# Gated columns' loads and first products half a column sooner, and the last tile's parts reordered at the entry of the up projection

## Chip, core and metric

The kernel runs on one core of a Trainium2 chip. The metric is device time in microseconds (us) of one execution; lower is better. The kernel before takes 1490.2 us, the median of three runs (1489.46 to 1492.07).

## What is computed

One encoder layer over 1024 tokens (two sequences of 512) of width 1024, in fp32. A projection of the normalised input gives attention heads, a state-space branch and two gates; the two branches are merged through the gates and projected, and a squared-ReLU MLP follows:

```python
y_att = windowed_attention(q, k, v, sink, bias, band_mask(seq_len))
y = jax.nn.gelu(lax.map(one_seq, u))                  # state-space branch
y_ssm = y * jax.nn.sigmoid(y @ w_glu + b_glu)
mixed = jax.nn.sigmoid(g_att) * y_att + jax.nn.sigmoid(g_ssm) * y_ssm
x = x + mixed @ w_out
h2 = rms_norm(x, ln2)
return x + jnp.square(jax.nn.relu(h2 @ w_up)) @ w_down
```

The change lies in two places: where `mixed` is made, and at the seam between `mixed @ w_out` with its norm and `h2 @ w_up`.

## The kernel before, in words

Every fp32 matmul is made of three: each operand is split into a high part (a cast to the matmul's format, on ScalarE, ACT) and a low part (what the cast left, a subtraction on VectorE, DVE). `mm3` (L113 to L117) multiplies high by high, high by low and low by high. A part is thus always a pair: an ACT cast, then a DVE subtraction that waits for it. TensorE is PE; its weight loads are PEld.

**The order.** From L1200 to L1714 the order of PE, ACT, DVE and GpSimd (POOL) is the order in which the program calls them (`written`). Each engine works its own queue in that order, and an instruction that waits holds back all behind it on its engine. The DMA issues of SyncE (SP) in this stretch are put in order by a scheduler, which issues a load when the tile that it writes comes free.

**The gated columns** (L1395 to L1461). The merge goes over eight columns m of 128 features, each in two halves s of 512 tokens. Column 0 is done ahead of the loop. For m = 1 to 7:

- `col.multiply` is 24 PE matmuls of y with column m of w_glu for half s (L758). At s = 0 of columns 2 to 6, `column_parts(m + 1)` splits the next column's weights, in two pieces: cast c_hi (L741) and subtraction c_lo (L742). Their raw pieces come by DMA (L740) into two buffers.
- `bank_out(m, s)` is ACT's sigmoid of the product (L1415).
- `late()` is the `mix` of the half before: DVE makes z (L1421, a product with the gate's tile gs, and L1422, the sum with at), ACT casts it into mixT (L1424), DVE subtracts (L1425). mixT is the moving side of the w_out projection that follows.
- `gate_in(m)` at s = 0: ACT's sigmoid of gs (L1409), DVE's product of gs with y (L1410, tile yr) and of at with ga (L1411), each over both halves.
- `loads(m + 1)` at s = 1 fetches the four tiles gs, yr, ga and at of the next column, 512 KB each (L1398, L1400, L1402, L1404). gs and yr have two buffers each, ga and at share four. So a tile of column m + 1 lands in the buffer of column m - 1: gs when L1421 of mix(m - 1, 1) is done, at when L1422 is, yr and ga when L1410 and L1411 of gate_in(m - 1) are.
- From m = 5 on, pieces of w_out are loaded (L1383) and split (cast L1391, subtraction L1392).

The last mix but one, mix(7, 0), makes the last eighth of what block 0 of the w_out projection reads (`Rows.block`, L1492, matmuls of 256 columns at L115 to L117).

**The entry of the up projection** (L1678 to L1718). The MLP's up projection is a product of 2 x 2 blocks in seven multiplications (Strassen's scheme in Winograd's form): B11, B21, B22 and T1 to T4 are blocks, or sums of blocks, of the normalised rows, and sums of blocks of w_up are their partners. Rows come in tiles of 128; the last of them (`last`) is normalised and transposed (`norm`, `turn`) while PE works on two products of r = 0 and two of r = 1 that need only B11 and B21, each 12 matmuls of 512 columns. Then PE multiplies, for r = 0, in this order: T2 with made[2], T3 with made[3], T1 with made[1], B22 with made[4], T4 with the raw block (L1795 to L1815). `put` writes a tile's part of one of the blocks (cast L1479, subtraction L1480), `parts` makes a pair of weight parts (u_hi, L1671; u_lo, L1672). Before the change, `last.old_rows()` (two sums, L1549), `first_sum` (copy L1657, sum L1659, relu, square) and the two sums of weights (L1696, L1697) come first; then `sums_a` casts B22, T1 and T2 and subtracts their low parts in this order, `between` makes made[2] and begins made[3], and T3, T4, made[1] and made[4] follow.

Of the kernel before, what the change touches and what calls it, by code (L numbers as in the profile page):

```python
# [23 lines left out]
KT = D // P  # L24
# [39 lines left out]
def hybrid_layer(ctx, tc, x, xT, rel, onehot, early, w_qkv, w_ug, q_gain, k_gain, sink,  # L64
# [1330 lines left out]
    with tc.tile_pool(name="glu", bufs=2, reuse_waits="tile") as gpool:  # L1395
# [11 lines left out]
        def gate_in(m):  # L1407
            gs_, yr, ga, at = gated[m]
            S.activation(gs_, gs_, AF.Sigmoid)  # L1409
            V.tensor_mul(gs_, gs_, yr)  # L1410
            V.tensor_mul(at, at, ga)  # L1411
# [25 lines left out]
        for m in range(1, KT):  # L1437
            col = ahead if m == 1 else Column(m)
            for s in range(NSEQ):
                col.multiply(max((s + 1) * 3 * KT - col.i, 0))  # L1440
                if s == 0 and 1 < m < KT - 1:
                    w_g[m + 1], subs = column_parts(m + 1)
                    for sub in subs:
                        sub()
                ending = m == KT - 1 and s
                if ending:
                    late()
                gl = bank_out(m, col.ps[s])
                if not ending:
                    late()  # L1450
                if s == 0:
                    gate_in(m)
                elif m < KT - 1:
                    gated[m + 1] = loads(m + 1)
                late = lambda m=m, s=s, gl=gl: mix(m, s, gl)
                if m >= 5:
                    n = (m - 5) * 2 + s
                    load_piece(n)
                    if 1 <= n < 5:
                        split_piece()  # L1460
# [17 lines left out]
    def put(dst, src, cs, at_once=True):  # L1478
        S.copy(dst[0][:, :, cs], src)  # L1479
        sub = lambda: V.tensor_sub(dst[1][:, :, cs], src, dst[0][:, :, cs].bitcast(F32))  # L1480
        return sub() if at_once else sub

    class Rows:
# [59 lines left out]
        def temp(self, name):  # L1543
            return rn2.tile([P, 4, P], F32, tag=name, name=name)

        def old_rows(self):
            self.s11, self.s21 = self.temp("s11"), self.temp("s21")
            for dst, (hi, lo) in ((self.s11, B11), (self.s21, B21)):
                V.tensor_add(dst, hi[:, :, self.cs].bitcast(F32), lo[:, :, self.cs].bitcast(F32))  # L1549

        def sums_a(self, between=None):
            cs, (x12, x22) = self.cs, self.xb
            b22 = put(B22, x22, cs, False)
            self.x22 = self.temp("x22")
            S.copy(self.x22, x22)
            self.t1, self.t2 = self.temp("tt0"), self.temp("tt1")
            V.tensor_sub(self.t1, x12, self.s11)
            t1 = put(T1, self.t1, cs, False)
            V.tensor_sub(self.t2, x22, self.t1)
            t2 = put(T2, self.t2, cs, False)  # L1560
            b22()
            t1()
            t2()
            if between:
                between()
            V.tensor_sub(self.t1, self.x22, x12)
            self.t3 = put(T3, self.t1, cs, False)

        def sums_b(self):
            self.t3()  # L1570

        def sums_c(self):
            V.tensor_sub(self.t2, self.t2, self.s21)
            put(T4, self.t2, self.cs)

    x1_all = slot_b.tile([P, NT // 2, D], F32, tag="act0", name="x1_all")
    with tc.tile_pool(name="wout", bufs=1, reuse_waits="tile") as wb:
# [30 lines left out]
        for t in range(1, 4):  # L1608
# [4 lines left out]
            if t > 1:  # L1613
                rows1[t - 2].sums_b()
                rows1[t - 2].sums_c()
            old.old_rows()
            old.norm()
            old.turn()
            add = rows1[t].half(1)
# [26 lines left out]
    def product(ps, w, b):  # L1646
        for k in range(4):
            mm3(ps, [q[:, k, :] for q in w], [q[:, k, :] for q in b], k == 0, k == 3)
        return ps

    def put_a(n, r, src):

        S.dma_start(a_scr[n - 1, :, r, :], src)

    def first_sum(r, p1, p2):
        u1 = up1.tile([P, HALF], F32, tag="u1", name="u1")
        S.copy(u1, p1)  # L1657
        a11 = up1.tile([P, HALF], F32, tag="a11", name="a11")
        V.tensor_add(a11, p2, u1)  # L1659
        S.activation(a11, a11, AF.Relu)  # L1660
        S.activation(a11, a11, AF.Square)
        put_a(1, r, a11)
        return u1, a11

    def sum_tile(i):
        return up1.tile([P, 4, P], F32, tag=f"s{i}", name=f"s{i}", bufs=1)
# [10 lines left out]

    begun, made = {}, {}  # L1678
    last = rows1[3]
    p1 = product(acc(), first[0][0], B11)  # L1680
    add()
    rows1[2].sums_b()
    rows1[2].sums_c()
    p2 = product(acc(), first[0][1], B21)
    last.norm()
    subs = [first_parts(up_raws[1][:, i], first[1][i]) for i in range(2)]
    for sub in subs:
        sub()
    last.old_rows()
    last.turn()  # L1690
    begun[0] = first_sum(0, p1, p2)
    p1 = product(acc(), first[1][0], B11)
    p2 = product(acc(), first[1][1], B21)
    a11_, a12_, a21_, a22_ = [up_raws[0][:, i] for i in range(4)]
    sm = [sum_tile(i) for i in range(4)]
    V.tensor_add(sm[0], a21_, a22_)  # L1696
    V.tensor_sub(sm[1], sm[0], a11_)  # L1697

    def between():
        made[2], sub = parts(sm[1], False)  # L1700
        sub()
        V.tensor_sub(sm[2], a11_, a21_)
        made[3], sub = parts(sm[2], False)
        last.sub3 = sub

    last.sums_a(between)
    last.sums_b()
    last.sub3()
    last.sums_c()
    made[1] = parts(sm[0])  # L1710
    V.tensor_sub(sm[3], a12_, sm[1])
    made[4] = parts(sm[3])
    begun[1] = first_sum(1, p1, p2)
    written.__exit__(None, None, None)  # L1714
    rn2_cm.__exit__(None, None, None)
    wb0_cm.__exit__(None, None, None)
# [265 lines left out]
```

## Time and profile before

| | |
|---|---|
| median of three runs | 1490.2 us (1489.46 to 1492.07) |
| the profiled execution | 1493.12 us, of which span 1491.3 us |
| PE busy | 1458.9 us, 98% of the span, 8070 matmuls |
| DVE busy | 1096.3 us, 74% |
| ACT busy | 764.2 us, 51% |
| gated columns' matmuls (L758), m = 1 to 7 | to 767.1 us |
| w_out projection and norm | 767.1 to about 884 us |
| up projection | from about 884 us |

Times in the trace count from the span's start. A row of the timeline has start, duration, engine, line, operation, the tile written and the tiles read (out<-in), the shapes, and in brackets the engine's idle time before it with what ended it. A wait row has total, number and longest. A row of the windows has the stretch, its length, each engine's busy time, the granted TensorE clock (1.00 is full speed), the DMA engines' mean busy share and the GB/s moved. Matmuls overlap in their rows: what counts is the distance from one start to the next.

### The profile page before, as it was taken

The page shows a single profiled execution, that of the slowest core. Times are in us where ns is not written, and L with a number is a line of the kernel's source. Part 1 is how long each engine was busy: PE and PEld are TensorE (multiplying, and loading weights), DVE is VectorE, ACT ScalarE, POOL GpSimd, SP SyncE. Part 2 cuts the span into 40 slices and gives each one's busy share as a digit, 9 for nine tenths or more (in the row PEclk, how much of TensorE's full clock was granted, in tenths as well). Part 3 has the DMA queues.
Part 4 walks back from the last instruction along what each step waited for, and adds up shares of the span by engine and source line. Part 5 has one row for each costly group of instructions (what it writes and reads, how often), then busy time and mean ns, then how long its engine had stood idle before and what let it go on. Part 6 is the DMA issues. An engine that isn't in the chain of part 4 may idle for free.

```text
span 1491.3 us, 22155 instructions
## 1 busy us (share of the span) xinstructions
PE 1458.9 (98%) x8070; PEld 1251.9 (84%) x8070; DVE 1096.3 (74%) x1835; ACT 764.2 (51%) x1366; POOL 168.4 (11%) x270
## 2 busy tenths in 40 slices
PE   6999999999999999999999999999999999999998
PEld 5888888888998888987879978888888888888787
DVE  7799979964637888888873689777777588575553
ACT  5589852224427777786433345555545543433332
POOL 4111120000322333333000100000000000000000
PEclk9999999999999999999999999999999999999999
DMA  8355566358841313236854125544443794454441
GB/s 297 109 177 172 173 214 234 133 180 282 269 119 56 100 58 93 74 127 232 274 199 144 71 96 181 161 151 153 155 155 127 269 350 161 148 181 154 127 126 59
DMA packets 129241, 243.91 MB, mean 164 GB/s; under 512 B 16059, under 2 KB 59323, under 8 KB 129132
## 3 DMA queue, kind: packets, MB, share of 16 engines
q1 hardware_dynamic: 104684, 186.87, 39.7%
q10 hardware_dynamic: 21888, 46.15, 8.2%
q0 software_dynamic: 2560, 9.48, 1.9%
q8 instruction: 64, 1.05, 0.3%
q14 instruction: 45, 0.37, 0.1%
HBM read 173.20 MB, written 81.82 MB: 171 GB/s over the span
## 4 chain that ended last, share of the span: by engine, by line
PE 81%; DVE 8%; issue 4%; ACT 3%; DMA 2%; POOL 1%; SPq 0%; DVEq 0%; ACTq 0%; POOLq 0%
PE bank L117 13%; PE bank L116 13%; PE bank L115 13%; PE acc L146 11%; PE acc L729 7%; PE acc L115 3%; PE acc L117 3%; PE acc L116 3%; PE sps L609 2%; PE sps L865 2%; PE sps L1053 2%; PE po L1085 2%; PE tps L1069 1%; DVE p L1057 1%; PE lag L624 1%
## 5 line engine op out<-in xcount | busy, mean ns | idle before, releaser
L116 PE MATMUL bank<-b_lo,a_hi 128*128 128x512 f32 x440 | 171.6, 390 | 1.9 <-DVE b_lo L1858 1.9
L117 PE MATMUL bank<-b_hi,a_lo 128*128 128x512 f32 x440 | 171.3, 389 | 0.0
L115 PE MATMUL bank<-b_hi,a_hi 128*128 128x512 f32 x440 | 170.7, 389 | 0.0
L729 PE MATMUL acc<-w_hi,hT 128*128 128x256 f32 x768 | 165.0, 292 | 0.0
L146 PE MATMUL acc<-hT,c_hi 128*128 128x512 f32 x512 | 161.2, 395 | 0.0
L1857 ACT CAST a_hi<-d_a 128x1024 fp32r<-128x1024 f32 x55 | 57.9, 1053 | 180.9 <-PE bank L116 177.7
L1858 DVE TENSOR_TENSOR a_lo<-d_a,a_hi 128x1024 fp32r<-128x1024 f32 x55 | 67.3, 1224 | 101.9 <-ACT a_hi L1857 99.9
L729 PEld LDWEIGHTS acc<-w_hi,hT 128*128 128x128 f32 x768 | 126.8, 190 | 1.7
L146 PEld LDWEIGHTS acc<-hT,c_hi 128*128 128x128 f32 x512 | 94.6, 188 | 21.1 <-issue 2.5
L729 PE MATMUL acc<-w_lo,hT 128*128 128x256 f32 x384 | 108.3, 282 | 0.0
L115 PE MATMUL bank<-act,u_hi 128*128 128x512 f32 x256 | 99.8, 390 | 1.1 <-ACT u_hi L1671 1.1
L146 PE MATMUL acc<-hT,c_lo 128*128 128x512 f32 x256 | 100.3, 392 | 0.0
L117 PE MATMUL bank<-act,u_lo 128*128 128x512 f32 x256 | 99.9, 390 | 0.2
L116 PE MATMUL bank<-act,u_hi 128*128 128x512 f32 x256 | 99.9, 390 | 0.1
L116 PEld LDWEIGHTS bank<-b_lo,a_hi 128*128 128x128 f32 x440 | 82.6, 188 | 19.8 <-DVE b_lo L1858 2.7
L117 PEld LDWEIGHTS bank<-b_hi,a_lo 128*128 128x128 f32 x440 | 82.6, 188 | 17.1
L115 PEld LDWEIGHTS bank<-b_hi,a_hi 128*128 128x128 f32 x440 | 82.6, 188 | 17.1
L1063 ACT ACTIVATE p<-p,nmx 128x257 f32<-128x257 f32 (+1 forms) x128 | 72.3, 565 | 35.9 <-DVE nmx L1057 35.4
L729 PEld LDWEIGHTS acc<-w_lo,hT 128*128 128x128 f32 x384 | 73.1, 190 | 2.4
L1057 DVE CUSTOM_DVE_ANT_0 p<-sps,bias,nsink 128x256 f32<-128x256 f32 (+1 forms) x128 | 69.2, 541 | 3.9 <-DMA bias<-line_scr 1.3
L115 PE MATMUL acc<-w,act 128*128 128x256 f32 (+1 forms) x224 | 68.8, 307 | 1.9 <-ACT act L1424 1.9
L1671 ACT CAST u_hi<-s 128x512 fp32r<-128x512 f32 x64 | 39.4, 622 | 60.6 <-PE bank L116 44.0
(369 smaller groups left out, 3737.5 us busy)
## 6 DMA issues: line engine op xcount, KB each, us to landing
d_a<-a_scr SPq DMA_DIRECT2D x55, 512.0 KB, 3.6
u_raw<-in_w_up_dram SPq DMA_DIRECT2D x32, 512.0 KB, 5.8
a_scr<-t ACTq DMA_DIRECT2D x64, 256.0 KB, 2.1
k<-in_w_down_dram SPq DMA_DIRECT2D x32, 512.0 KB, 5.6
a_scr<-a ACTq DMA_DIRECT2D x48, 256.0 KB, 3.3
c_raw<-in_w_ug_dram SPq DMA_DIRECT2D x44, 256.0 KB, 3.4
ct_scr<-ctab SPq DMA_DIRECT2D x16, 576.0 KB, 3.3
ctab_in<-ct_scr SPq DMA_DIRECT2D x32, 288.0 KB, 4.7
```

Source lines behind the costliest of these rows:

```text
L115: PE.matmul(ps, a[0], b[0], start=first, stop=False)
L116: PE.matmul(ps, a[0], b[1], start=False, stop=False)
L117: PE.matmul(ps, a[1], b[0], start=False, stop=last)
L146: PE.matmul(self.ps[s], self.w[p == 2][:, k, :], hT[s][p == 1][:, k, :], start=i % (3 * KT) == 0, stop=i % (3 * KT) == 3 * KT - 1)
L609: PE.matmul(ps[:, i * P:(i + 1) * P], bm[:, ri, g, :], u_sb[:, g, :], start=True, stop=True)
L729: PE.matmul(ps, act[p == 2][:, k, col:col + P], self.w[k // 4][p == 1][:, k % 4, :], start=i == 0, stop=i == 3 * KT - 1)
L865: PE.matmul(o, ctab[:, ri, gi, 0:T * CH], st[:, ri, g].rearrange("p s k -> p (s k)"), start=False, stop=ri == 1)
L1057: V.tensor_tensor_reduce(self.p[:, h, 1:1 + self.nk], self.s[h][:, 0:self.nk], biases[self.j][h][:, b0:b0 + self.nk], -1.0, nsink[:, hh:hh ...
L1063: S.activation(p, p, AF.Exp, bias=self.nmx[:, h:h + 1], scale=-1.0, accum_out=self.sums[:, h, self.qb:self.qb + 1])
L1671: S.copy(hi, src)
L1857: S.copy(hi, src)
L1858: V.tensor_sub(lo, src, hi.bitcast(F32))
```

## The change

In the gated columns, `gate_in(m + 1)` moves to s = 1 of column m (column 1 keeps its place, and column 2's follows half a column later), and `loads(m + 1)` to s = 0. At the entry of the up projection, the last tile's sums and parts are written out by hand in the order in which PE reads them: T2 and made[2] first, then T3 and made[3], T1 and made[1], B22, then T4 and made[4]. The sum sm[0] goes ahead of the low part of T4 of the tile before, ReLU and square of r = 0 and the copy of r = 1's first product go behind B22's cast, and the two sums of `old_rows` are apart, s11 for T2 early and s21 for T4 late. x22 is copied out of PSUM after T2's cast, and B22's part is made from the copy.

```diff
@@ -1449,9 +1449,12 @@
                 if not ending:
                     late()
                 if s == 0:
-                    gate_in(m)
+                    if m == 1:
+                        gate_in(1)
+                    if m < KT - 1:
+                        gated[m + 1] = loads(m + 1)
                 elif m < KT - 1:
-                    gated[m + 1] = loads(m + 1)
+                    gate_in(m + 1)
                 late = lambda m=m, s=s, gl=gl: mix(m, s, gl)
                 if m >= 5:
                     n = (m - 5) * 2 + s
@@ -1543,12 +1546,14 @@
         def temp(self, name):
             return rn2.tile([P, 4, P], F32, tag=name, name=name)
 
-        def old_rows(self):
-            self.s11, self.s21 = self.temp("s11"), self.temp("s21")
-            for dst, (hi, lo) in ((self.s11, B11), (self.s21, B21)):
+        def old_rows(self, *which):
+            for i in which:
+                name, (hi, lo) = (("s11", B11), ("s21", B21))[i]
+                dst = self.temp(name)
+                setattr(self, name, dst)
                 V.tensor_add(dst, hi[:, :, self.cs].bitcast(F32), lo[:, :, self.cs].bitcast(F32))
 
-        def sums_a(self, between=None):
+        def sums_a(self):
             cs, (x12, x22) = self.cs, self.xb
             b22 = put(B22, x22, cs, False)
             self.x22 = self.temp("x22")
@@ -1561,17 +1566,15 @@
             b22()
             t1()
             t2()
-            if between:
-                between()
             V.tensor_sub(self.t1, self.x22, x12)
             self.t3 = put(T3, self.t1, cs, False)
 
         def sums_b(self):
             self.t3()
 
-        def sums_c(self):
+        def sums_c(self, at_once=True):
             V.tensor_sub(self.t2, self.t2, self.s21)
-            put(T4, self.t2, self.cs)
+            return put(T4, self.t2, self.cs, at_once)
 
     x1_all = slot_b.tile([P, NT // 2, D], F32, tag="act0", name="x1_all")
     with tc.tile_pool(name="wout", bufs=1, reuse_waits="tile") as wb:
@@ -1613,7 +1616,7 @@
             if t > 1:
                 rows1[t - 2].sums_b()
                 rows1[t - 2].sums_c()
-            old.old_rows()
+            old.old_rows(0, 1)
             old.norm()
             old.turn()
             add = rows1[t].half(1)
@@ -1652,15 +1655,25 @@
 
         S.dma_start(a_scr[n - 1, :, r, :], src)
 
-    def first_sum(r, p1, p2):
+    def first_copy(p1):
         u1 = up1.tile([P, HALF], F32, tag="u1", name="u1")
         S.copy(u1, p1)
+        return u1
+
+    def first_sum(r, p1, p2):
+        return first_rest(r, first_copy(p1), p2)()
+
+    def first_rest(r, u1, p2):
         a11 = up1.tile([P, HALF], F32, tag="a11", name="a11")
         V.tensor_add(a11, p2, u1)
-        S.activation(a11, a11, AF.Relu)
-        S.activation(a11, a11, AF.Square)
-        put_a(1, r, a11)
-        return u1, a11
+
+        def rest():
+            S.activation(a11, a11, AF.Relu)
+            S.activation(a11, a11, AF.Square)
+            put_a(1, r, a11)
+            return u1, a11
+
+        return rest
 
     def sum_tile(i):
         return up1.tile([P, 4, P], F32, tag=f"s{i}", name=f"s{i}", bufs=1)
@@ -1677,40 +1690,59 @@
 
     begun, made = {}, {}
     last = rows1[3]
+    a11_, a12_, a21_, a22_ = [up_raws[0][:, i] for i in range(4)]
+    sm = [sum_tile(i) for i in range(4)]
     p1 = product(acc(), first[0][0], B11)
     add()
     rows1[2].sums_b()
-    rows1[2].sums_c()
+    t4_put = rows1[2].sums_c(False)
+    V.tensor_add(sm[0], a21_, a22_)
+    t4_put()
     p2 = product(acc(), first[0][1], B21)
     last.norm()
     subs = [first_parts(up_raws[1][:, i], first[1][i]) for i in range(2)]
     for sub in subs:
         sub()
-    last.old_rows()
+    V.tensor_sub(sm[1], sm[0], a11_)
+    u1 = first_copy(p1)
     last.turn()
-    begun[0] = first_sum(0, p1, p2)
+    made[2], made2 = parts(sm[1], False)
+    last.old_rows(0)
+    x12, x22 = last.xb
+    cs = last.cs
+    tt0, tt1 = last.temp("tt0"), last.temp("tt1")
+    V.tensor_sub(tt0, x12, last.s11)
+    V.tensor_sub(tt1, x22, tt0)
+    t2 = put(T2, tt1, cs, False)
+    rest0 = first_rest(0, u1, p2)
+    made2()
+    t2()
     p1 = product(acc(), first[1][0], B11)
     p2 = product(acc(), first[1][1], B21)
-    a11_, a12_, a21_, a22_ = [up_raws[0][:, i] for i in range(4)]
-    sm = [sum_tile(i) for i in range(4)]
-    V.tensor_add(sm[0], a21_, a22_)
-    V.tensor_sub(sm[1], sm[0], a11_)
-
-    def between():
-        made[2], sub = parts(sm[1], False)
-        sub()
-        V.tensor_sub(sm[2], a11_, a21_)
-        made[3], sub = parts(sm[2], False)
-        last.sub3 = sub
-
-    last.sums_a(between)
-    last.sums_b()
-    last.sub3()
-    last.sums_c()
-    made[1] = parts(sm[0])
+    x22c = last.temp("x22")
+    S.copy(x22c, x22)
+    V.tensor_sub(sm[2], a11_, a21_)
+    V.tensor_sub(last.s11, x22c, x12)
+    made[3], made3 = parts(sm[2], False)
+    t3 = put(T3, last.s11, cs, False)
+    made3()
+    t3()
+    t1 = put(T1, tt0, cs, False)
+    made[1], made1 = parts(sm[0], False)
+    t1()
+    made1()
+    b22 = put(B22, x22c, cs, False)
+    begun[0] = rest0()
+    u1 = first_copy(p1)
+    last.old_rows(1)
+    b22()
+    V.tensor_sub(tt1, tt1, last.s21)
+    t4_put = put(T4, tt1, cs, False)
     V.tensor_sub(sm[3], a12_, sm[1])
-    made[4] = parts(sm[3])
-    begun[1] = first_sum(1, p1, p2)
+    made[4], made4 = parts(sm[3], False)
+    t4_put()
+    made4()
+    begun[1] = first_rest(1, u1, p2)()
     written.__exit__(None, None, None)
     rn2_cm.__exit__(None, None, None)
     wb0_cm.__exit__(None, None, None)
```

The subtraction order of the other tiles is as it was; `old_rows(0, 1)` there makes both sums.

## The prediction

> **What bounds the kernel now.** I read the page first, then the waits of PE, then windows and the timeline at the two places where PE waits inside the changed code, and last the DMA issues there. The page gives the span; the profiled execution took 1493.12 us, 1.8 us more than its span and 2.9 us more than the median 1490.2 of the three timed runs. I take the gains and losses in microseconds from this execution and apply them to the median.
>
> ```profile
> span 1491.3 us, 22155 instructions
> ```
>
> PE is the bound almost everywhere. Asked for PE's waits between 690 and 800 us, and between 865 and 925 us, the trace names three, and these are all the changed code can win back:
>
> ```profile
> PE acc L115 <- ACT act L1424: 1.9, 1, 1.9
> PE acc L116 <- DVE w L1392: 1.7, 1, 1.7
> ```
> ```profile
> PE bank L115 <- ACT u_hi L1671: 1.1, 1, 1.1
> ```
>
> The first two lie at one place, the entry of the w_out projection. The windows there (span, PE busy, granted clock, DMA share, GB/s) and PE's timeline show that the place costs more than the waits:
>
> ```profile
> 769.40:773.60 4.20, 0.64 (x4) 0.93 0.20 44
> 773.60:779.80 6.20, 6.15 (x27) 0.50 0.97 364
> ```
> ```profile
> 767.11 0.28 PE L115 MATMUL acc<-w,act 128*128 128x256 f32 x1
> 767.22 0.28 PE L116 MATMUL acc<-w,act 128*128 128x256 f32 x1
> ...
> 779.85 0.28 PE L115 MATMUL acc<-w,act 128*128 128x256 f32 x1
> ```
>
> The projection starts at 767.11, and its 49th matmul at 779.85. The trace has 0.12 us from one such matmul to the next at full clock, so 48 of them are 5.76 us and the 49th was due at 772.87: 6.98 us are lost. 3.6 us are the two waits. After them 27 matmuls run from 773.65 to 779.85 at a clock of 0.50: 6.20 us where 27 x 0.12 = 3.24 would do, 2.96 us more. The remaining 0.4 us is the restart around each wait. So the lost clock is nearly half of the loss, and it follows a stretch of 4.2 us in which PE worked 0.64 us.
>
> What ends last there is the chain of DVE and ACT through the gated columns. This is half a round of it, for m = 5 (the row with x2 is two instructions):
>
> ```profile
> 742.61 1.29 DVE L742 TENSOR_TENSOR c_lo<-c_raw,c_hi 128x512 fp32r<-128x512 f32 x2
> 743.81 1.14 DVE L1421 TENSOR_TENSOR z<-gl,gs 128x512 f32<-128x512 f32 x1
> 744.98 0.69 DVE L1422 TENSOR_TENSOR z<-z,at 128x512 f32<-128x512 f32 x1
> 746.36 0.69 DVE L1425 TENSOR_TENSOR act<-z,act 128x512 fp32r<-128x512 f32 x1 [0.69 <-ACT act L1424]
> 747.32 1.23 DVE L1410 TENSOR_TENSOR gs<-gs,yr 128x1024 f32<-128x1024 f32 x1 [0.27 <-ACT gs L1409]
> 748.47 1.22 DVE L1411 TENSOR_TENSOR at<-at,ga 128x1024 f32<-128x1024 f32 x1
> 749.60 1.14 DVE L1421 TENSOR_TENSOR z<-gl,gs 128x512 f32<-128x512 f32 x1
> ```
> ```profile
> 772.98 0.62 ACT L1424 CAST act<-z 128x512 fp32r<-128x512 f32 x1 [4.25 <-DVE z L1422]
> ```
>
> DVE's idle in it is the 0.69 us of each mix and 0.27 us before L1410, both inside fixed sequences; it never waits for PE. DVE runs late on its own work, and PE gets the last hi part at 773.60.
>
> **Part 1, the gated columns.** Nothing is added or removed; gate_in(m + 1) (one ACT sigmoid, L1410, L1411) moves from behind mix(m, 1) to behind mix(m, 0), and the four loads from (m, 1) to (m, 0). All seven gate_in still stand ahead of mix(7, 0) on DVE, each behind an L1425 as now, with the same 0.27 us of waiting for the sigmoid. So the length of DVE's chain up to L1424 at 772.98 is the same sum in another order: worth 0.0 us by itself. The earlier product buys nothing, because DVE has no hole that it could fill.
>
> What the move does change is what stands behind gate_in. From L1425 at 746.36 to L1421 at 749.60 are 3.24 us; L742's two halves start 0.60 apart, and L1425 has their shape, so gate_in takes 3.24 - 0.60 = 2.64 us. The weight parts c_lo of the next column now stand behind it and come 2.64 us later. Column 4 has the least room:
>
> ```profile
> 722.31 1.28 DVE L742 TENSOR_TENSOR c_lo<-c_raw,c_hi 128x512 fp32r<-128x512 f32 x2
> ```
> ```profile
> 724.04 0.39 PE L758 MATMUL acc<-act,c_lo 128*128 128x512 f32 x1
> ```
>
> Its first half is done at 722.31 + 0.69 = 723.00 and is read at 724.04: 1.04 us of room, so PE waits 2.64 - 1.04 = 1.6 us there, a wait that is not in the trace of before. It costs nothing in the end: PE arrives at 767.11 + 1.6 and stands so much less at the entry, since the chain's end is fixed. Bounds: 0 to 1.6 us, taken as 0 net.
>
> The loads have a price. gs(m + 1) can be fetched only when L1421 of mix(m - 1, 1) has freed its buffer; call that L1421's start t. Now L1409 of gate_in(m + 1) wants it after mix(m - 1, 1) and mix(m, 0): the next L1421 at t + 3.15 (746.36 + 0.60 - 743.81), L1422 1.17 later, L1424 0.73 after that, L1409 0.52 behind it: t + 5.57. SP's queue of before, near the same rows:
>
> ```profile
> 743.32 0.94 SPq L740 DMA_DIRECT2D c_raw<-in_w_glu_dram  x2
> 744.98 0.33 SPq L1398 DMA_DIRECT2D gs<-gs_scr  x1
> 745.70 0.33 SPq L1404 DMA_DIRECT2D at<-mix_scr  x1
> 748.58 0.32 SPq L1400 DMA_DIRECT2D yr<-y_scr  x1
> 749.71 0.32 SPq L1402 DMA_DIRECT2D ga<-ga_scr  x1
> ```
> ```profile
> DMA to landing us min/median/max: 3.4/4.3/4.7
> ```
>
> The second fence is L1398's landing. The SP issues stand in the order in which DVE frees the buffers: yr and ga behind L1410 and L1411, c_raw behind L742, gs and at behind L1421 and L1422. With gate_in moved, L1410 ends at t - 1.20 - 1.13 - 1.15 + 1.23 = t - 2.25, so yr and ga of the column after go out just ahead of c_raw and gs instead of 4 us behind them, on the same queue: 0.524 x 4 = 2.10 MB up to the end of gs. The rates of full stretches:
>
> ```profile
> 704.00:712.00 8.00, 8.00 (x37) 6.63 (x36) 7.13 (x9) 2.25 (x4) 1.22 (x2) 1.00 0.96 297
> 712.00:716.00 4.00, 4.00 (x19) 3.31 (x18) 3.28 (x3) 0.76 (x2) 3.16 (x2) 1.00 0.92 352
> ```
>
> Their last two columns are DMA share and GB/s. The fastest landing, 3.4, less 0.524 MB at 352 GB/s (1.5 us) leaves 1.9 us fixed. So gs lands at t - 2.2 + 1.9 + 6.0 = t + 5.7 at 352 GB/s, or t + 6.8 at 297: 0.1 to 1.2 us after L1409 wants it. Behind L1409 wait L741, the next sigmoid and L1424 on ACT, L1410, c_lo and the mix on DVE, and PE for c_lo. This meets gate_in(3) to gate_in(6); gate_in(2) has its gs from 704, and for gate_in(7) a split piece gives 0.6 us and no c_raw is left. Four times 0.1 to 1.2 is 0.4 to 4.8 us; below nothing it cannot be, as a load cannot speed up DVE. I take 0.3 each, nearer to the row of 352 since the other shares the engines with a POOL load: **+1.2 us**.
>
> [...]
>
> **Part 2, the up half's entry.** PE should go on from 883.42 at 0.23 us a matmul:
>
> ```profile
> 883.42 0.39 PE L117 MATMUL acc<-act,f 128*128 128x512 f32 x1
> 884.94 0.49 PE L115 MATMUL bank<-act,u_hi 128*128 128x512 f32 x1 [1.13 <-ACT u_hi L1671]
> ...
> 889.69 0.39 PE L115 MATMUL bank<-act,u_hi 128*128 128x512 f32 x1
> ```
> ```profile
> 883.02 0.69 DVE L1559 TENSOR_TENSOR tt<-sps,tt 128x512 f32<-128x512 f32 x1 [0.91 <-ACT x L1555]
> 883.63 0.68 DVE L1480 TENSOR_TENSOR act<-sps,act 128x512 fp32r<-128x512 f32 x1
> 884.23 1.28 DVE L1480 TENSOR_TENSOR act<-tt,act 128x512 fp32r<-128x512 f32 x2
> 885.43 0.68 DVE L1672 TENSOR_TENSOR u_lo<-s,u_hi 128x512 fp32r<-128x512 f32 x1
> ```
>
> Sixteen steps from 883.42 to 889.69 take 6.27 us instead of 3.63 (0.227 each, the pace of the rows around): 2.64 us lost, in the first product's T2 and u parts and in the second's u_lo. B22 and T1, which are used third and fourth, stand ahead of T2 on DVE. Now they go behind. The new order counted from here:
>
> ```profile
> 875.89 1.28 DVE L1528 SCALAR_TENSOR_TENSOR rn_xn<-x,rs,ln_bc 128x1024 f32<-128x1024 f32 x1
> 877.09 1.29 DVE L1476 TENSOR_TENSOR f<-u_raw,f 128x512 fp32r<-128x512 f32 x2
> 878.29 1.29 DVE L1549 TENSOR_TENSOR s<-act,act 128x512 f32<-128x512 f32 x2
> ```
>
> The norm stays at 875.89, as sm[0] fills the wait for T4's cast ahead of it. From 878.29 at 0.60 each: sm[1], s11, tt0, tt1 (880.1), a11, u_lo (881.3), T2's lower part at 881.9, done at 882.6. ACT's casts, 0.62 each, follow sm[1] at 879.0 and tt1 at 880.8, in time for both. PE wants them at 883.65: 1.0 us of cover. The second product needs T3 and its u_lo at 886.4; sm[2], the T3 sum, u_lo and T3's lower part with one cast between end at about 885.2. So the whole loss goes: **-2.6 us** (bounds 0 and -2.6). relu and square of a11 and the copy of p1 go behind on ACT; their readers come after the first products. What is late next is made[4] for the fourth product, done near 890.2 and wanted at 891.8.
>
> **Sum.** -2.6 + 0.0 + 1.2 = -1.4 us: 1491.7 by the profiled execution, 1488.8 by the median. About 0.2%, 3.0 us, is what a measurement of this kernel can tell from no change, so this is no change.
>
> **The rivals.** *The clock stays whole (faster).* If gs lands in time, PE's 1.6 us at column 4 shrink the standing at the entry from two waits to one of about 2 us: L116's split, ready at 771.2, is met at 767.11 + 1.6 + 19 x 0.12 = 771.0. For it speaks that the stop of 1.5 us at 883.42 left the pace at 0.23; against it that less than 1 us of lateness closes it again, since lateness pushes the chain's end and PE alike. Then the 2.96 us of half clock go: -2.6 - 3.0 = -5.6, **1484.6**. Chance 0.36.
>
> [...]
>
> *The loads come late (slower).* At 297 GB/s gs is 1.2 us late four times, and mix_scr's store of 0.5 MB falls among the loads of gate_in(3), 1.8 us more: +6.6 - 2.6 = +4.0, **1494.2**. It decides from 5.6 us of lateness in all. For it speaks the median landing of 4.3 with only c_raw ahead; against it the row of 352. Chance 0.18.
>
> *The entry does not clear.* Were ACT late with T2 by over 1 us, PE's wait stays: -1.4 + 2.6 = +1.2, **1491.4**. The cover of 1.0 us speaks against it. Chance 0.04. My forecast has 0.42.
>
> **The numbers.** Faster by over 0.2% (below 1487.2) is the first rival and a little of the forecast where the loads come near the lower bound: 0.37. Within: the rest of the forecast and the third rival: 0.45. Slower: 0.18. The forecast's own range is 1487.2 to 1491.2 (lateness 0 to 3.6 us). Both signs hold much of the chance, so the range takes in the first rival to 0.8 us below and most of the second: 1483.8 to 1493.8.
>
> **What would show it.** Right: no wait for u_hi L1671 near 884 and the second product at 0.23 us a matmul; idle of DVE before L1410 grown from 0.27 to about 0.6; PE waits for c_lo L742 at the columns' starts; the clock at 0.50 again behind the entry. The first rival: a clock of 1.00 there. The second: idle before L1410 over 1.5. The prediction is wrong if DVE's chain from L1410 of m = 1 to the last L1424 gets shorter than now without a change of the clock.

## The result and the profile after

The changed kernel takes 1496.52 us, the median of five runs (1495.46 to 1498.10); the kernel before, run beside it, 1490.87 (1489.46 to 1495.11). The ratio is 1.0035, with a 95% interval of 1.0023 to 1.0048: slower, by 0.0035 x 1490.87 = 5.2 us. The profiled execution took 1498.1 us, and its span is 5.0 us longer than that of before:

```profile
span 1496.3 us, 22154 instructions
```

Both traces hold the same 8070 matmuls in the same order, so the start of each can be taken from its start in the other. The changed kernel is 1.3 us ahead when the gated columns begin, 4.6 behind once column 3 runs, 4.3 behind after the entry of w_out, 1.6 behind after the up half's entry, 4.0 behind at the end of the up projection, and 5.0 behind at the end. (The last 1.0 us arises in the down projection, at one wait that moved from kernel to kernel below by 0.8 us the one way to 1.3 the other, with the same code there; I do not put it down to the change.) So the gated columns lost 5.6 us, the up half's entry won 2.7, and r = 1 gave 2.4 of it back.

PE's waits of the changed kernel, asked for 690 to 800 us (the four longest) and for 800 to 940 us:

```profile
PE acc L758 <- DVE c_lo L742: 3.9, 1, 3.9
PE acc L115 <- ACT act L1424: 1.9, 1, 1.9
PE acc L115 <- ACT w L1391: 0.6, 1, 0.6
PE acc L116 <- DVE w L1392: 0.4, 1, 0.4
```
```profile
PE bank L115 <- ACT u_hi L1684: 1.2, 1, 1.2
PE bank L117 <- DVE u_lo L1685: 0.7, 1, 0.7
```

The entry of w_out still has its wait for L1424. New is a stop of 3.9 us in the columns, for c_lo. The waits near 884 us are gone; the two in the second fence stand at 902, in r = 1.

**The gated columns.** DVE's timeline where the stop arises (start, duration; the bracket is the idle time ahead):

```profile
703.42 1.22 DVE L1410 TENSOR_TENSOR gs<-gs,yr 128x1024 f32<-128x1024 f32 x1
...
711.17 1.22 DVE L1410 TENSOR_TENSOR gs<-gs,yr 128x1024 f32<-128x1024 f32 x1 [2.25 <-DMA yr<-y_scr]
712.31 3.36 DVE L1411 TENSOR_TENSOR at<-at,ga 128x1024 f32<-128x1024 f32 x1
715.60 1.28 DVE L742 TENSOR_TENSOR c_lo<-c_raw,c_hi 128x512 fp32r<-128x512 f32 x2
```

This is gate_in(2). c_lo of column 3, which in the kernel before ran ahead of all this, starts at 715.60. What gate_in(2) waits for is in the rows of ACT, SP and POOL:

```profile
710.08 1.06 ACT L1409 ACTIVATE gs<-gs 128x1024 f32<-128x1024 f32 x1 [1.89 <-DMA gs<-gs_scr]
```
```profile
703.53 0.33 SPq L1398 DMA_DIRECT2D gs<-gs_scr  x1
```
```profile
703.27 1.22 POOL L1119 DMA_DIRECT2D fac<-rs_scr  x2 [5.55 <-DMA rs_scr<-row]
711.28 3.31 POOL L1124 TENSOR_TENSOR ya<-ya,fac 128x1024 f32<-128x1024 f32 x1 [6.80 <-DMA fac<-rs_scr]
```

gs(2) is issued at 703.53 and lets the sigmoid start at 710.08, 6.5 us later, beside POOL's loads of fac. Then L1411 runs into POOL's product at 711.28 and takes 3.36 us instead of 1.22. This meeting is not new: in the kernel before POOL's product met L1422, which took 2.65 us instead of 0.69:

```profile
712.56 2.65 DVE L1422 TENSOR_TENSOR z<-z,at 128x512 f32<-128x512 f32 x1
```

So it costs the chain 2.1 us instead of 2.0. What is new is that c_lo of column 3 stands behind it, and behind the late gs.

The columns behind it wait too; here is gate_in(5):

```profile
744.98 1.06 ACT L1409 ACTIVATE gs<-gs 128x1024 f32<-128x1024 f32 x1 [0.87 <-DMA gs<-gs_scr]
```
```profile
738.29 1.13 DVE L1421 TENSOR_TENSOR z<-gl,gs 128x512 f32<-128x512 f32 x1
...
746.08 1.22 DVE L1410 TENSOR_TENSOR gs<-gs,yr 128x1024 f32<-128x1024 f32 x1 [1.24 <-ACT gs L1409]
```

Its gs was issued at 739.45, which is 36.0 us behind the first L1410. In the kernel before the same load went out 30.1 us behind it (734.83 against 704.76), with 11.4 us to go until its sigmoid; now there are 5.5:

```profile
739.45 0.32 SPq L1398 DMA_DIRECT2D gs<-gs_scr  x1
```
```profile
734.83 0.33 SPq L1398 DMA_DIRECT2D gs<-gs_scr  x1
```

So the change made this load later, not sooner: its buffer comes free behind L1421 of mix(3, 1), and gate_in(4) now stands ahead of that.

Over all columns, the idle time of DVE ahead of L1410, after and then before:

```profile
  ACT gs L1409: 4.3, 5
  DMA yr<-y_scr: 2.3, 1
```
```profile
  ACT gs L1409: 1.6, 6
```

That is 6.6 us against 1.6. (The trace puts the 2.25 us of column 2 down to yr, but yr(2) was issued at 694.46, and the sigmoid of gs ended at 711.14, just ahead of L1410 at 711.17; in kernel 1 below the same wait is named gs, with 2.61.) The chain ends here, in ACT's row of mix(7, 0):

```profile
777.22 0.62 ACT L1424 CAST act<-z 128x512 fp32r<-128x512 f32 x1 [2.57 <-DVE z L1422]
```

From the first L1410 to this row are 777.22 - 703.42 = 73.80 us. In the kernel before the first L1410 is

```profile
704.76 1.22 DVE L1410 TENSOR_TENSOR gs<-gs,yr 128x1024 f32<-128x1024 f32 x1
```

and the row of the prediction ends the chain at 772.98: 68.22 us. The chain is 5.6 us longer, 5.0 of it idle time ahead of L1410. The windows of the changed kernel (span, busy time and count of PE, PEld, DVE, ACT, POOL, then granted clock, DMA share, GB/s) show the two stops and the clock behind each:

```profile
711.60:716.30 4.70, 0.74 (x2) 0.30 (x2) 4.70 (x4) 1.15 (x3) 3.77 (x2) 0.95 0.46 177
716.30:719.40 3.10, 3.07 (x8) 2.45 (x9) 2.38 (x4) 0.76 (x2) 0.00 (x0) 0.52 1.01 309
...
772.90:777.90 5.00, 2.10 (x15) 1.49 (x13) 3.60 (x6) 1.82 (x4) 0.00 (x0) 0.94 0.32 86
777.90:784.10 6.20, 6.20 (x27) 5.98 (x28) 4.69 (x7) 2.19 (x4) 0.00 (x0) 0.50 0.94 365
```

**The up half's entry.** PE's rows:

```profile
887.66 0.39 PE L117 MATMUL acc<-act,f 128*128 128x512 f32 x1
887.89 0.39 PE L115 MATMUL bank<-act,u_hi 128*128 128x512 f32 x1
...
892.65 0.39 PE L115 MATMUL bank<-act,u_hi 128*128 128x512 f32 x1
```
```profile
901.26 0.39 PE L117 MATMUL bank<-t,f_lo 128*128 128x512 f32 x1
902.81 0.50 PE L115 MATMUL bank<-act,u_hi 128*128 128x512 f32 x1 [1.16 <-ACT u_hi L1684]
903.15 0.39 PE L116 MATMUL bank<-act,u_hi 128*128 128x512 f32 x1
904.21 0.50 PE L117 MATMUL bank<-act,u_lo 128*128 128x512 f32 x1 [0.67 <-DVE u_lo L1685]
```

The first products run on at 0.23 us a matmul. Five products later PE stops for r = 1's u_hi. On ACT this cast stands behind f_hi, the first part of r = 2, which waits for its load:

```profile
901.62 0.62 ACT L1478 CAST f_hi<-u_raw 128x512 fp32r<-128x512 f32 x1 [4.46 <-DMA u_raw<-in_w_up_dram]
902.14 1.65 ACT L1684 CAST u_hi<-s 128x512 fp32r<-128x512 f32 x3
```

In the kernel before the two stood in the same order, but the wait was short:

```profile
896.95 0.62 ACT L1475 CAST f_hi<-u_raw 128x512 fp32r<-128x512 f32 x1 [0.73 <-DMA u_raw<-in_w_up_dram]
```

The load waits for its buffer, until f_lo of r = 0 has read it: f_lo ran at 892.40 before and at 895.74 after, and the load went out at 893.11 and at 896.46. PE is 1.6 us behind there, so against PE part 2 itself sent this load 1.75 us later.

### The profile page after: what moved, and what is told of

The parts are those of the page before. It is cut to its first block, busy times and chain, and to the rows that moved or that the text cites. A ratio compares the mean times of both kernels' runs of the same rounds, so it can differ in the third digit from the quotient of the medians.

```text
span 1496.3 us, 22154 instructions
## 1 busy us (share of the span) xinstructions
PE 1462.2 (98%) x8070; PEld 1253.6 (84%) x8070; DVE 1096.5 (73%) x1835; ACT 764.7 (51%) x1366; POOL 169.2 (11%) x270
## 4 chain that ended last, share of the span: by engine, by line
PE 81%; DVE 8%; DMA 4%; issue 3%; ACT 2%; POOL 1%; SPq 0%; DVEq 0%; ACTq 0%; POOLq 0%
PE bank L117 13%; PE bank L116 13%; PE bank L115 13%; PE acc L146 11%; PE acc L729 7%; PE acc L115 3%; PE acc L117 3%; PE acc L116 3%; PE sps L609 2%; PE po L1085 2%; PE sps L1053 2%; PE sps L865 2%; PE tps L1069 2%; PE lag L624 1%; DMA gs<-gs_scr 1%
```

## The experiments

Each kernel ran in five rounds against the kernel before on the same chip; the medians of before are 1491.6, 1491.7 and 1491.7 us in the three groups. Intervals are 95%.

**Theory and rivals.** Theory A: part 1 loses because gs lands late, most of all for column 2, and DVE's chain grows by the waits; part 2 wins at its place and gives the gain back in r = 1. Rival B: the sooner order or the sooner loads cost by themselves. (In the expectations of kernels 1 to 3 the letter B stands for other rivals, which are told there.) Later came theory C against D, on why part 2 gives its gain back, and E and G, on the entry of w_out.

**1. Part 1 alone** (the first hunk of the change).

> Gated columns moved, entry of the up projection as before. Theory A (gs lands after its sigmoid wants it, first at gate_in(2), then at gate_in(4) to gate_in(6); the weight parts of column 3 stand behind that): all of the changed kernel's loss is here, 1490.9 + 5.5 = about 1496.4, PE's wait for c_lo at column 3 near 4 us, and L1424's last hi part about 5.5 us later than in the kernel before. Theory B (the loss comes from the new order at the up projection's entry and after it): 1490.9 to 1491.5, and the chain's end where it was.

Measured: 1498.49 us, ratio 1.0039 (1.0025 to 1.0053). The stop at column 3 is 3.9 us again, and L1409's waits for its load in this kernel are

```profile
  DMA gs<-gs_scr: 4.4, 4
```

Part 1 makes the whole loss, 5.8 us.

**2. Part 2 alone** (all other hunks).

> Gated columns as before, entry of the up projection in the new order. Theory A (the 2.6 us won at the entry are given back at r = 1, where the casts u_hi stand on ACT behind a cast that waits for the load of r = 2): -2.6 + 2.1 = -0.5, about 1490.4, with one PE wait of about 1.2 for u_hi some 15 us behind the entry. Theory B (that wait comes from the gated columns' lateness and not from the new order): -2.6, about 1488.3, without that wait.

Measured: 1492.31 us, ratio 1.0000 (0.9991 to 1.0009): nothing, though the up half's entry wins 2.7 us in the trace. PE's waits between 860 and 940 us and ACT's rows there:

```profile
PE bank L115 <- ACT u_hi L1681: 2.0, 1, 2.0
PE bank L117 <- DVE u_lo L1682: 0.7, 1, 0.7
```
```profile
895.47 0.62 ACT L1475 CAST f_hi<-u_raw 128x512 fp32r<-128x512 f32 x1 [5.36 <-DMA u_raw<-in_w_up_dram]
895.99 1.66 ACT L1681 CAST u_hi<-s 128x512 fp32r<-128x512 f32 x3
```

r = 2's f_hi waits 5.36 us ahead of r = 1's casts. Behind the 2.0 and 0.7 us the matmuls go at 0.43 us from 898.06 to 901.05, at a mean granted clock of 0.73 over 896 to 901, so r = 1 gives back 4.9 us in this one execution, more than the two waits and more than the 2.7 won; over all executions part 2 comes out even.

**3. Part 1 with column 2 at its old place.**

```diff
                 if s == 0:
-                    gate_in(m)
-                elif m < KT - 1:
-                    gated[m + 1] = loads(m + 1)
+                    if m <= 2:
+                        gate_in(m)
+                    if m < KT - 1:
+                        gated[m + 1] = loads(m + 1)
+                elif 1 < m < KT - 1:
+                    gate_in(m + 1)
```

> Gated columns moved but for column 2, whose gate_in stays at its old place; entry of the up projection as before. Theory A: the 2.0 us of DVE at gate_in(2) and PE's stop of 4 us at column 3 with the halved clock are gone, and 0.9 us each at gate_in(4) to gate_in(6) stay, with 0.1 us more between mixes: chain +3.4, about 1494.2. Theory B (gate_in(2) with its stop is the whole loss, the later loads are hidden): about 1490.9.

Measured: 1495.27 us, ratio 1.0022 (1.0013 to 1.0032). The stop at column 3 is gone; two columns still wait, 2.4 us for gs in all. Column 2 carries somewhat under half of the loss.

**4. The calls of the loads half a column sooner, every gate_in at its old place.**

```diff
                 if s == 0:
                     gate_in(m)
-                elif m < KT - 1:
-                    gated[m + 1] = loads(m + 1)
+                    if m < KT - 1:
+                        gated[m + 1] = loads(m + 1)
```

> Only the loads are called half a column sooner; gate_in and the entry as before. Theory A (loads cost only where the products wait for them): the chain's end where it was, 1490.9 within 0.5. Theory B (the bunched loads themselves take bandwidth or SP's queue from c_raw and w_raw): at least 1 us slower, 1492 or more, with ACT waiting for DMA at L741 or L1391.

Measured: 1491.68 us, ratio 1.0005 (0.9996 to 1.0014). L1409 never waits for its load. But the loads themselves do not go out sooner, because each still waits for its buffer. This is gs(6), 40.13 us behind the first L1410 (703.88); in the kernel before it stands 40.22 behind it:

```profile
744.01 0.33 SPq L1398 DMA_DIRECT2D gs<-gs_scr  x1
```

Of the loads of the four tiles behind the first L1410 only at(3) moves by more than 0.2 us, by 2.0. So this kernel shows that moving the calls alone moves next to nothing. What sooner loads cost it does not show; that half of rival B is met by kernel 7.

**5. Part 2 alone, with r = 2's first part held behind r = 1's casts.** One ACT copy of four columns ties f_hi of r = 2 to the third of the parts that r = 1 makes; the real cast overwrites it.

```diff
-        def raw_parts(src):
+        def raw_parts(src, after=None):
...
+            if after is not None:
+                S.copy(hi[:, 0, 0:4], after[:, 0, 0:4])
...
-                u1, a11 = first_sum(r, product(bank(), raw_parts(raw[:, 0]), B11), product(bank(), raw_parts(raw[:, 1]), B21))
+                u1, a11 = first_sum(r, product(bank(), raw_parts(raw[:, 0], mark if r == 2 else None), B11), product(bank(), raw_parts(raw[:, 1]), B21))
...
-            p5 = product(bank(), w1(), T1)
+            w1p = w1()
+            mark = w1p[0]
+            p5 = product(bank(), w1p, T1)
```

> Kernel: the one before with part 2 alone (as in the run of part 2 alone), and the first parts of r = 2 held behind r = 1's own casts by one added ACT copy of 4 columns, so that the load of u_raw(2) no longer stands in ACT's and DVE's queues ahead of u_hi and u_lo of r = 1. Theory C (part 2 gains its 2.5 us at the entry and gives it back only because f_hi of r = 2 waits 5.36 us for its load ahead of the three u_hi casts): the ACT wait for u_raw ahead of u_hi is gone, the PE waits at r = 1's p6 (2.0 and 0.7 us, and the halved clock behind them) go, and the gain stays: 1488 to 1489.5, ratio 0.9975 to 0.9990, faster. Rival D (r = 1's parts are late for their own reasons, DVE and ACT being full behind the entry): PE waits of 1 to 3 us at the same place and 1491 to 1492.5, ratio 0.9995 to 1.001.

Measured: 1488.73 us, ratio 0.9982 (0.9973 to 0.9991). ACT's rows have changed places:

```profile
892.60 1.66 ACT L1681 CAST u_hi<-s 128x512 fp32r<-128x512 f32 x3 [0.45 <-ACT a L1669]
...
897.10 0.62 ACT L1475 CAST f_hi<-u_raw 128x512 fp32r<-128x512 f32 x1 [2.60 <-DMA u_raw<-in_w_up_dram]
```

The load is still waited for, but by nobody whom PE needs, and PE has no wait between 860 and 940 us. Theory C holds.

**6. Part 1 with a third buffer for gs.** ga and at share three buffers instead of four to make room.

```diff
-            gs_ = evp.tile([P, T, NSEQ, NCHUNK], F32, tag="ev", name="gs")
+            gs_ = (gpool if m % 3 == 2 else evp).tile([P, T, NSEQ, NCHUNK], F32, tag="g3" if m % 3 == 2 else "ev",
+                                                      name="gs", bufs=1 if m % 3 == 2 else 2)
...
-            ga = gpool.tile([P, NTOK], F32, tag="ga", name="ga", bufs=4)
+            ga = gpool.tile([P, NTOK], F32, tag="ga", name="ga", bufs=3)
...
-            at = gpool.tile([P, NTOK], F32, tag="ga", name="at", bufs=4)
+            at = gpool.tile([P, NTOK], F32, tag="ga", name="at", bufs=3)
```

> Kernel: the one before with part 1 alone, and a third buffer for gs (the ga and at loads share three buffers instead of four to make room), so that no gs load has to wait for the last reader of gs two columns back. Theory A (part 1 loses because gs lands late, most of all for column 2): the sigmoid L1409 waits for no DMA (under 0.3 us in each column, instead of 2.25, 1.12, 0.56 and 0.50), the PE stop of 3.9 us ahead of column 3 is at most 1 us, and the time is back at that of the kernel before or a little under it: 1488 to 1492.5, ratio 0.998 to 1.0006. Rival B (the sooner products themselves cost: they run beside POOL's product and push c_lo back): L1409 waits for nothing and the time stays at 1496 to 1499, ratio 1.003 to 1.005. Between: 1493 to 1495.5, both have a share.

Measured: 1493.37 us, ratio 1.0011 (1.0001 to 1.0021): 4.2 of the 5.8 us are gone, which is the case between theory A and rival B. No sigmoid waits for gs any more. The stop that I expected to vanish did not; its cause is another load:

```profile
PE acc L758 <- DVE c_lo L742: 3.7, 1, 3.7
```
```profile
713.75 1.31 DVE L1412 TENSOR_TENSOR at<-at,ga 128x1024 f32<-128x1024 f32 x1 [3.34 <-DMA at<-mix_scr]
```
```profile
705.79 0.32 SPq L1405 DMA_DIRECT2D at<-mix_scr  x1
```

This load of at(2) is 8 us under way, behind gs and yr of column 3 and beside fac. In the changed kernel it went out at 695.41; here, with three buffers for ga and at, it has to wait until L1412 of gate_in(1) is done with one, at 705.76. So this stop comes from the buffer that I took away to make room, and not from part 1: gs(2), with its third buffer, was in time: its sigmoid ran at 708.10 with no wait ahead, where the changed kernel's ran at 710.08 behind a wait of 1.89 us. The 3.34 us lengthen the chain by only 2.1 (table below), since DVE sits most of them out beside POOL's product (711.64 to 713.98), and its meeting with that product had cost it 2.0 in the kernel before.

**7. Part 1 with both edits: column 2 at its old place, three buffers for gs.**

> Kernel: part 1 alone with column 2's sigmoid and products left at their old place and a third buffer for gs: no gs load should be late and no column should stop. Theory A (part 1's loss is the late loads and the stop at column 3 alone; DVE works through the columns without idle time, so the order of its work by itself is worth nothing): L1409 and the at product wait for no DMA by over 0.3 us, no PE wait over 1 us ahead of a column, and the time is that of the kernel before: 1490.5 to 1492.5, ratio 0.999 to 1.0006. Rival G (with the loads in time the sooner products shorten the chain into the entry of w_out, and the clock stays whole there): 1486 to 1489, ratio 0.996 to 0.998. Rival B (the sooner products cost by themselves): 1494 to 1497.

Measured: 1493.18 us, ratio 1.0007 (0.9998 to 1.0016), against 1.0039 of part 1. The time lies between the ranges of theory A (up to 1492.5) and rival B (from 1494). The longest wait ahead of a column is 1.0 us, and the chain is as long as before. The seven kernels of the columns in one table, with the first L1410, the L1424 of mix(7, 0), and what lies between:

| kernel | first L1410 | L1424 | chain, us | L1409 waits for gs, us | ratio |
|---|---|---|---|---|---|
| before | 704.76 | 772.98 | 68.22 | 0 | 1 |
| the change | 703.42 | 777.22 | 73.80 | 4.5 | 1.0035 |
| 1, part 1 | 704.26 | 778.12 | 73.86 | 4.4 | 1.0039 |
| 3, column 2 old | 703.37 | 773.77 | 70.40 | 2.4 | 1.0022 |
| 6, third buffer | 703.41 | 773.70 | 70.29 | 0 (at: 3.3) | 1.0011 |
| 7, both edits | 703.31 | 771.62 | 68.31 | 0 | 1.0007 |
| 4, calls only | 703.88 | 772.03 | 68.15 | 0 | 1.0005 |

The chains come from one execution each, which lies up to 2.3 us off its kernel's median (kernel 7's is 2.3 us under it); the ratios are of medians. With that reserve the time follows the chain. With its waits taken away the new order is worth nothing that can be told from zero, as theory A says; G's 3 to 5 us are not there, and as the interval ends at 1.0016, or 2.4 us, most of part 1's 5.8 us is no cost of the order. Whether the 0.07% that are left are a cost of the order or of the measurement is open; kernel 10 below shows the same 0.07% against kernel 5.

**8. The kernel before with the last two mixes exchanged**, mix(7, 0) ahead of mix(6, 1).

```diff
                 if ending:
                     late()
+                    kept()
                 gl = bank_out(m, col.ps[s])
-                if not ending:
+                if m == KT - 1 and not s:
+                    kept = late
+                elif not ending:
                     late()
```

> Kernel: the one before, with the last two mixes in the other order (column 7 of the first sequence ahead of column 6 of the second), nothing of the change in it. Theory E (the end of the DVE chain through the gated columns sets the entry of w_out, as the step on the clock supposed): the last hi cast that the entry waits for comes some 3.2 us sooner (one mix of z, z, lo), the entry's PE waits shrink from 3.6 us to under 1, the clock is not halved behind it, and the time falls by 3.2 to 6 us: 1485.5 to 1488.5, ratio 0.996 to 0.998. Rival F (the entry waits for something else too, such as the w_out parts, or the waits come back at the half's second entry): ratio 0.999 to 1.001.

Measured: 1491.50 us, ratio 0.9998 (0.9988 to 1.0008): rival F. The entry of w_out does come sooner, and the next block of w_out takes it back:

```profile
PE acc L115 <- ACT w L1391: 1.9, 1, 1.9
PE acc L115 <- ACT act L1424: 1.4, 1, 1.4
```
```profile
783.20:785.20 2.00, 0.17 (x2) 0.00 (x0) 0.00 (x0) 0.59 (x1) 0.00 (x0) 1.00 1.00 401
785.20:788.80 3.60, 3.26 (x14) 2.99 (x15) 1.33 (x3) 0.64 (x2) 0.00 (x0) 0.53 0.34 123
```

The wait of 1.9 us is for a piece of w_out that is still being loaded at 401 GB/s, and behind it the granted clock is 0.53 for 3.6 us, down from 1.00.

**9. Kernel 5 with the exchange of kernel 8.**

> Kernel: part 2 alone with r = 2's first parts held back, and the two last mixes swapped: the two edits of the runs beside it together. If both theories hold and their gains add: 1483 to 1486, ratio 0.9945 to 0.9965. If only the swap holds: 0.996 to 0.998; if only the held-back parts: 0.9975 to 0.999; if a gain at the entry of w_out is given back at the up half's entry (its cover then being shorter): no better than the better of the two alone.

Measured: 1487.18 us, ratio 0.9971 (0.9960 to 0.9983), the fastest here and faster than both kernels of the case. Kernel 5 ran beside it: only two of its eleven runs (1487.41 and 1487.78) lie below the highest of the six of kernel 9 (1488.05). So here the exchange does add about 1.5 us, which it did not do by itself in kernel 8. In kernel 9's trace the granted clock is 1.00 from 767.0 to 773.0 and from 777.4 to 789.0 us; in kernel 8's it is 0.86 from 767.5 to 773.5, 0.76 from 773.5 to 777.0 and 0.53 from 785.2 to 788.8. That this is the reason is not tested.

**10. The whole change with the edits of 5 and 7.**

> Kernel: the whole change with three edits: column 2 at its old place, a third buffer for gs, and r = 2's first parts held behind r = 1's casts. By theories A and C it is the mended part 2 (1488.7, ratio 0.998) with a part 1 that is worth nothing: 1487.5 to 1490, ratio 0.997 to 0.999. By G the two gains add: 1483 to 1486. By B it is slower than the mended part 2 by 3 to 5 us.

Measured: 1490.12 us, ratio 0.9989 (0.9980 to 0.9998): part 2's gain with a part 1 that brings nothing.

**11. Kernel 10 with the exchange of kernel 8.**

> Kernel: the run beside it with the last two mixes swapped too. The mended part 2 gained 1.5 us more by the swap (1488.7 to 1487.2): by A and C 1486 to 1488.5, ratio 0.996 to 0.998. If the chain into the entry is already short (G), the swap adds nothing to the run beside it.

Measured: 1488.14 us, ratio 0.9977 (0.9968 to 0.9986), in the expected range. That is 2.0 us below kernel 10, which ran beside it and whose interval (0.9980 to 0.9998) does not hold 0.9977; so the exchange adds something here too.

**12. The kernel before with the hold of kernel 5 alone.**

> Kernel: the one before with r = 2's first parts held behind r = 1's casts and nothing of the change: what the holding back is worth by itself. In the kernel before, f_hi waits 0.73 us for its load and the PE waits 1.1 us for u_hi there. By theory C: 0.5 to 1.5 us gained (1490 to 1491.2, ratio 0.999 to 0.9997), so that part 2's order is worth 1.5 to 2.5 us of the 2.9 that the two gained together. If the holding back alone gives the whole 2.9 (1488.5 to 1489.2), part 2's order is worth nothing.

Measured: 1491.44 us, ratio 0.9998 (0.9990 to 1.0007). The hold by itself is worth nothing, part 2 by itself is worth nothing, and the two together are worth 0.18%: part 2's gain is real and needs the way cleared behind it. The 0.5 us at least that I expected of the hold did not show. I had put PE's wait of 1.1 us for u_hi down to r = 1; it stands at the up half's entry, ahead of what the hold touches, and is still there in this kernel.

## Why the prediction was wrong

**What bounds the kernel, and the order of part 1: right.** DVE's chain through the columns ends last; 5.6 us more of it cost 5.2 to 5.8 us. The new order by itself is worth 0.0 as forecast (68.31 against 68.22 us, kernel 7), to within the 0.07% that stay open there.

**The step that failed is the price of the loads**, "Four times 0.1 to 1.2 is 0.4 to 4.8 us ... I take 0.3 each": +1.2 forecast, +5.0 measured in DVE's idle time ahead of L1410. It failed twice. First, "gate_in(2) has its gs from 704": 704 is when its load is issued, not when it lands. I gave this load no price, although the row of 297 GB/s that I quoted held POOL's load of fac as well (0.52 MB on its own queue, 17.8% of the DMA engines' time from 704 to 716 us). It costs 2.25 - 0.27 = 2.0 us, and beside it lies the stop of 3.9 us. Second, I chose the wrong end of the bounds. For gate_in(5), with t = 738.29, gs lets the sigmoid go at 744.98, t + 6.7, where I gave t + 5.7 to t + 6.8 and took nearly the lower. DVE's idle time there is 1.24 us instead of 0.27, a price of 0.97; I had said that 0.6 would be seen, and that over 1.5 would speak for the slower rival. Column 3, which I counted among the four, had its tiles in time, so three columns near the upper bound and one column that I had left out make up the 5.0.

**SP's order** was not quite what I wrote: at and gs went out ahead of c_raw, and ga last. Up to the end of gs that is 1.57 MB and not the 2.10 that I counted, so that t + 6.7 lies so near to my upper bound is in part luck. That gs lands behind all that was issued ahead of it was my estimate. No run here shows it, and none tells it from a mere sharing of the bandwidth.

**PE's wait for c_lo** came at column 3 with 3.9 us, not at column 4 with 1.6. I had counted only the 2.64 us of gate_in ahead of c_lo; at column 3 the late gs (2.0) and the meeting with POOL's product (2.1), which c_lo ran ahead of before, came on top. That PE "stands so much less at the entry" is what happened: 4.6 us behind after the stop, and 4.3 after the entry.

**The first rival, a clock that stays whole, did not happen**: behind the entry it is 0.50 for 6.2 us. That one stop of about 2 us would keep the clock was my estimate, and its ground, the stop of 1.5 us at 883.42 that left the pace at 0.23, does not reach so far: in kernel 8 the clock is 0.53 behind one stop of 1.9 us. The stops that the traces show, and the clock behind each, stand in the last section.

**The slower rival was the true one in kind.** I gave it 1494.2 us and a chance of 0.18, deciding "from 5.6 us of lateness in all", and my range ended at 1493.8, below it. Its terms were not the true ones either: its 1.8 us at gate_in(3) did not come (0.27 us of idle time there, as before), and the 2.0 at gate_in(2) it did not have. The chain grew by 5.6, which with the -2.7 of part 2 makes +2.9; the other 2.4 are what r = 1 gave back, which neither forecast nor rival had. The sum, 5.6 - 2.7 + 2.4 = 5.3, stands beside the 5.2 that were measured.

**Part 2: the entry was right, the net was not.** -2.6 was forecast and -2.7 measured there, and no product waits. "What is late next is made[4]" was the error: made[4] came in time, and r = 1's u_hi was late, behind a load that I had not followed into the stretch where the scheduler orders ACT, and whose buffer the new order freed 1.75 us later against PE. Kernels 2, 5 and 12 show it: 1.0000 alone, 0.9982 with the way cleared.

## What to carry to other kernels

A load has its price where it lands, not where it is issued (gs(2) was issued at 703.53, and its sigmoid began at 710.08): when a reader is moved ahead, follow the landing of every tile that it reads, above all the first round's, which meets other traffic than the steady state (here POOL's load of fac). Where the buffer count says when a load may start, moving the call of the load moves next to nothing (gs(6) in kernel 4: 40.13 us behind the first L1410 instead of 40.22), and moving its reader ahead shortens the time in which it can land (gs(5): 5.5 us instead of 11.4); a third buffer took away most of the loss (4.2 of 5.8 us), though the buffer that made room for it cost a stop of its own. So ask of a new buffer what it takes away. In both parts a load went out later because the change had put the last reader of its buffer further back (L1421 for gs(5), f_lo for r = 2). And when a stall is cleared, look for the next wait beyond the stretch that was edited, at an instruction that waits for a load in front of the work that PE needs.

## What the hardware showed that was not expected

- **The clock halved behind some short stops and not behind others.** Behind one stop of 1.9 us (kernel 8) the granted clock was 0.53 for 3.6 us; behind one of 1.9 us in kernel 7 it was 0.61 on the mean from 772.2 to 776.2. In kernel 2 stops of 2.0 and 0.7 us had matmuls at 0.43 us behind them, while in the changed kernel stops of 1.16 and 0.67 us within 1.4 us left them at 0.23, with a clock of 1.00 from 902.7 to 906.5. In the kernel before the stop of 1.1 us near 884 left it at 1.00.
- **The clock came down while PE stood, and not at one length of stop.** In the changed kernel it was 0.50 from 715.75 to 719.16 us and from 777.25 to 784.08, 3.4 and 6.8 us; in the kernel before from 772.96 to 779.78, 6.8 us. At the first it fell 3.3 us into the stop of 3.9; at the other two 1.2 us into a stop of 1.9, in a stretch with shorter stops ahead (0.6 and 0.4 us in the changed kernel, 1.7 in the one before). What sets the moment these runs do not show.
- **A DVE product that met POOL's took longer.** L1411 took 3.36 us instead of 1.22 when it began 1.0 us into POOL's product of 3.31 us; it ended at 715.67, 1.1 us behind POOL's product, which ended at 714.59. In the kernel before L1422, begun 0.3 us into POOL's product of 2.39 us, took 2.65 us instead of 0.69 and ended 0.5 us behind it. Why it took longer no run shows.
- **512 KB took 3.3 to 8.1 us to land** in these columns of the changed kernel (gs, yr, ga and at, from 693 to 790 us), and 3.4 to 8.3 in the kernel before, with other loads under way. In kernel 6 at(2) was read 8.0 us behind its issue, beside POOL's load of fac; whether fac held it up was not tested.
